# Another offset for the modulated input, merged small operations in the second attention, and a new schedule for the conditioning loads

## The chip, the cores and the metric

The kernel runs on one core of one Trainium2 chip, as a single launch. The metric is the time of one execution on the device in microseconds (us). A time is a median over several executions; for the kernel before it is 2225.2 us, the median of 3 runs (2223.86, 2225.2 and 2228.75). A profile is one further execution, recorded by the hardware profiler, with a time and a span of its own. The engines are named as the profile names them: PE is TensorE's matmuls and PEld its weight loads, DVE is VectorE, ACT is ScalarE, POOL is GpSimd, SP is SyncE.

## The reference, cut to what matters

A trunk of two layers over 256 positions of 2048 channels, all in float32. Layer 0 mixes positions with a forgetting attention of 16 heads of 128, layer 1 with a sliding-window attention of 32 query heads of 64 in pairs on 4 key heads, with one sink logit a head; after each stands a gated feed-forward with a causal convolution of width 3 (5632 wide). Every sub-layer is modulated by vectors that come from the conditioning vector c: shift and scale ahead of it, a gate behind it.

```python
def swa_attention(h, pos, w_in, sinks, w_o):
    ...
    sink = jnp.broadcast_to(sinks.astype(jnp.float32).reshape(1, 1, Hk, G, 1, 1), s.shape[:-1] + (1,))
    p = jax.nn.softmax(jnp.concatenate([s, sink], axis=-1), axis=-1)[..., :-1].astype(v.dtype)
    o = jnp.einsum('bnhgqk,bnkhd->bnqhgd', p, vb).reshape(B, S, Hq * dh)
    return o @ w_o
...
    c_act = jax.nn.silu(c)
    for i in range(DEPTH):
        mod = c_act @ ada_w[i] + ada_b[i]
        sh1, sc1, g1, sh2, sc2, g2 = jnp.split(mod[:, None, :], 6, axis=-1)
        h = x * (1.0 + sc1) + sh1
        ...
        x = layer_norm(DEEPNORM_ALPHA * x + (1.0 + g1) * y, ln_mix_g[i], ln_mix_b[i])
        h = x * (1.0 + sc2) + sh2
        y = conv_ffn(h, ffn_w_up[i], ffn_conv_w[i], ffn_conv_b[i], ffn_w_down[i])
        x = layer_norm(DEEPNORM_ALPHA * x + (1.0 + g2) * y, ln_ffn_g[i], ln_ffn_b[i])
    return x
```

## The kernel before, in words

**Matmuls.** Every float32 operand of a large matmul is split into a high part (rounded to the matmul's own format) and the remainder. The product of two operands is then three matmuls: high by high, high by low, low by high. mm() (line 75) issues each of them, so nearly all of TensorE's rows in the profile have line 75 and are told apart by tile names: wh and wl are the two parts of a weight tile, hH and hL those of the modulated input h, gT those of the feed-forward's hidden values, oT those of the attention's output; ws and xs are the results.

**Weights.** stream() (from line 256) brings the weights in tiles of 512 KB, two blocks of 128 rows by 512 columns: a DMA on SP's queue (line 261), ScalarE's rounding copy to wh (264), VectorE's subtraction to wl (275). It queues a "go" for each tile, which runs two tiles later and issues that tile's matmuls: 24 of 128x256 where the weights are the stationary operand (w_stationary, tile ws, with hH and hL moving: the up-projections and the first attention's queries and keys), or 12 of 128x512 where the activations are (x_stationary, tile xs: the other projections, with hH as a stationary operand in the second attention's input projection). then() puts other work into the same queue in its order, such as a change of a rate or the step between two sub-layers. Each go first runs one step of every deferred evacuation (run_post), and ends with tick(): the conditioning planner, and one step of the background work (later(), step(), drain()).

**hH and hL** share one buffer, hpad (line 483). hH begins 40 floats (160 bytes) into it and hL follows; hpad itself begins at a multiple of 256 bytes in its partition. Weight tiles, gT, oT and the like lie 224 bytes behind such a multiple.

**turn()** (326 to 329) issues four transposes of the identity into a bank that nobody reads. w_stationary calls it once, ahead of the third weight tile, in the first column block of each sub-block of a feed-forward: for the first sub-block it's in the second of the block's two projections, for the second sub-block in the first.

**The conditioning planner** works through the vectors in the order of ada_list (374); (l, v) is layer l and v of 0 to 5, where 2 and 5 are gates (used as rows) and the others columns. Its rate is a number of calls per weight tile; ada_tick() adds it to a debt and calls ada_step() for each whole one. ada_vector() (from 380) needs 32 calls that each issue a load of 512 KB (398) on SP's queue and one step on VectorE over 128x1024 (402 or 404). A gate then needs 5 calls more (with 2 ahead, one with its bias load on POOL), in which TensorE sums over the partitions and ScalarE copies (412 to 416). A column vector needs 4 calls that each transpose four pieces (442) and let ScalarE sum along them (446), and 2 that finish it (HELD, with another way, is empty). ada_need() calls ada_step() as often as it takes until a vector is there.

**Rates.** First feed-forward: 0.64 in the up-projections, 0.78 in the down-projections, second feed-forward 0.4 in both. Second attention: 0.3 for its keys and values (set behind between()), then 0.9 to the end of its output projection. The first attention's output projection: 1.3.

**between()** (from 1132) stands ahead of each sub-layer but the first: ada_need for shift and scale, spin() (some matmuls that nobody reads, to bridge a gap), then modulate(): normalise() (652, 654), transposes, and mod_pair() (503 to 508), which writes hH and hL. In residual() (626 to 643) the two blocks of 128 rows are added to x, with bn_stats and, on GpSimd, the power of -1/2.

**The second attention.** swa() (from 974) projects keys and values, then four groups of queries; evac_q() (1004 to 1023) rotates and transposes a group and hands its four pairs of heads to the background work; there are 16 pairs in all. A pair() (from 1025) computes the scores of both heads, calls probs() for each, turned() (three transposes and a copy to pT, 727 to 733) for each, and multiplies by the values; its result goes to an o_tile (the last four are hH's and hL's own blocks 12 to 15). probs() (692 to 713) takes the maximum (VectorE), two exponentials with sums (ScalarE), with a sink the exponential es of the sink (ScalarE) and its addition to ss (VectorE), the reciprocal (VectorE), and two scalings of pr by it (ScalarE, line 713: one 128 wide, one 256 wide). The first attention calls probs() too, without a sink. Its yields mark the steps that the background work is spread over. out_proj() (from 744) follows, with a wait in stat() that runs background steps until the o_tile that it needs is there.

**conv_ffn()** (from 1065) handles its 11 column blocks in two sub-blocks of 6 and 5: up-projection with convolution (1072 to 1075), silu and product, then the down-projection of the sub-block. Ahead of the first down-projection the background work is drained; ahead of each, ada_need asks for the gate.

Of the kernel before, what the change touches and what calls it, by code (L numbers as in the profile page):

```python
# [10 lines left out]
F32 = mybir.dt.float32  # L11
# [30 lines left out]
def hybrid_trunk(ctx: ExitStack, tc: tile.TileContext, a: dict, out: bass.AP):  # L42
# [283 lines left out]
    def turn():  # L326
        o = bank("turn")
        for j in range(4):
            pin(nc.tensor.transpose(o[:, j * P:(j + 1) * P], ident, ident))

    def w_stationary(wsrc, col, turn_at=-1):

        ps = w_banks()

        def use(kc, h, l):
            if kc == turn_at:
                turn()
            w_mm(ps, kc, h, l)

        stream(wsrc, 0, col, list(range(KC)), use)  # L340
        return ps
# [142 lines left out]
    hH, hL = (hpad[:, 40 + a * KC * S:40 + (a + 1) * KC * S].rearrange("p (k s) -> p k s", s=S) for a in range(2))  # L484
# [207 lines left out]
    def probs(S_ps, skc=None, nskc=None):  # L692

        regs = ((0, P), (P, 3 * P))
        nm = sp.tile([P, 2], F32, tag="nm", name="nm")
        pr = f32(gtile("pr")).rearrange("p a b -> p (a b)")[:, :3 * P]
        ss = sp.tile([P, 2], F32, tag="ss", name="ss")
        for r, (b, e) in enumerate(regs):

            mk = mask[:, 2:3, :] if r == 0 else (mask[:, 0::2, :] if skc is None else mask[:, 1:3, :])  # L700
            nc.vector.tensor_tensor_reduce(pr[:, b:e].rearrange("p (a k) -> p a k", k=P),
                                           S_ps[:, b:e].rearrange("p (a k) -> p a k", k=P), mk, -1.0,
                                           -NEG if skc is None else nskc, ALU.add, ALU.min, nm[:, r:r + 1])
        for r, (b, e) in enumerate(regs):
            nc.scalar.activation(pr[:, b:e], pr[:, b:e], AF.Exp, bias=nm[:, r:r + 1], scale=-1.0,
                                 accum_out=ss[:, r:r + 1])
        if skc is not None:
            es = sp.tile([P, 2], F32, tag="es", name="es")
            nc.scalar.activation(es, nm, AF.Exp, bias=skc)
            nc.vector.tensor_tensor(ss, ss, es, op=ALU.add)  # L710
        nc.vector.reciprocal(ss, ss)
        for r, (b, e) in enumerate(regs):
# [3 lines left out]
    def attend(scores, outputs, sinks=()):  # L716
# [4 lines left out]
        pr = probs(sps, *sinks)  # L721
# [22 lines left out]
    def out_proj(oT, full, w_o, l):  # L744
# [11 lines left out]
        for i, ks in enumerate((range(0, 8), range(8, 12))):  # L756
            then(lambda i=i: ada.update(rate=((1.3, 1.3, 1.3, 1.3), (0.9,) * 4)[l][i]))
            for d in range(2):
                part(d, list(ks))
        then(lambda: ada_need(l, 2))  # L760
        for d in range(D // WB):
            if d < 2:
                part(d, list(range(12, KC)))
            else:
                then(lambda d=d: ada.update(rate=((1.3, 1.3, 1.3, 1.3), (0.9,) * 4)[l][d]))
# [208 lines left out]
    def swa(l, j):  # L974
# [50 lines left out]
        def pair(g, n, q):  # L1025
# [11 lines left out]
            yield  # L1037
            prs, pTs = [], []
# [148 lines left out]
```

## Time and profile before

| | |
|---|---|
| median of 3 runs | 2225.2 us (2223.86 to 2228.75) |
| profiled execution | 2228.91 us |
| its span | 2227.1 us |
| mean granted TensorE clock | 0.992 |
| TensorE matmul busy | 2174.6 us, 98% |
| TensorE weight load busy | 1981.6 us, 89% |
| VectorE busy | 1778.1 us, 80% |
| ScalarE busy | 1167.2 us, 52% |
| GpSimd busy | 19.0 us, 1% |
| read from HBM | 598.37 MB, 270 GB/s |

The span is the time from the first to the last recorded instruction; the execution's own time is 1.8 us longer. Busy times are sums over the span, of one profiled execution. Matmuls run in a pipeline, so a matmul's recorded duration is longer than the time from one to the next; the rate is read from their number in a stretch. The stages on the span's clock: opening to 188 us, first attention's projections to 378, its output projection to 478, modulation to 500, first feed-forward: up to 747, down to 880, up to 1103, down to 1208; second attention: input projections from 1215 to 1364, output projection to 1481, modulation to 1518; second feed-forward: up to 1755, down to 1886, up to 2104, down to 2214; the rest is the last normalising and the output.

### The profile page before, as it was taken

How to read it: one execution, taken by the hardware profiler on the slowest of the kernel's cores; microseconds unless marked ns; L12 is line 12 of the kernel's file. 1: busy time of each engine (PE TensorE's matmuls, PEld its weight loads, DVE VectorE, ACT ScalarE, POOL GpSimd, SP SyncE). 2: the span in 40 equal slices, each digit the busy share in tenths (PEclk: the TensorE clock that was granted, in tenths of full speed). 3: DMA queues.
4: the chain of work that ended last, by engine and by line, in shares of the span. 5: the costliest groups of instructions: out<-in, count | busy, mean ns of one | idle time of the engine just before them, and what ended most of it. 6: DMA issues, size and time to landing. Idle time of an engine off the chain costs nothing. (4 is left out here: it accounts for less than half of the span.)

```text
span 2227.1 us, 38402 instructions
## 1 busy us (share of the span) xinstructions
PE 2174.6 (98%) x14931; PEld 1981.6 (89%) x14931; DVE 1778.1 (80%) x2426; ACT 1167.2 (52%) x1873; POOL 19.0 (1%) x48
## 2 busy tenths in 40 slices
PE   6999999999999999999999999999999999999997
PEld 5999888889999988999987777789999888999986
DVE  6978999979979968789888988769888555666756
ACT  3435655555555543555634578745555533555532
POOL 0000000000000000000000000000000000000000
PEclk9999999999999999999999999999999999999999
DMA  9999999969979989889887877658888566666663
GB/s 334 377 349 356 349 349 329 328 225 327 347 249 315 317 287 341 272 289 327 276 305 288 281 237 235 217 170 297 270 273 266 183 195 191 194 193 196 193 192 110
DMA packets 274248, 603.00 MB, mean 271 GB/s; under 512 B 21063, under 2 KB 29961, under 8 KB 273553
## 3 DMA queue, kind: packets, MB, share of 16 engines
q1 hardware_dynamic: 273008, 595.85, 78.8%
q0 software_dynamic: 1056, 4.69, 0.6%
q8 instruction: 117, 1.92, 0.3%
q14 instruction: 67, 0.54, 0.1%
HBM read 598.37 MB, written 2.10 MB: 270 GB/s over the span
## 5 line engine op out<-in xcount | busy, mean ns | idle before, releaser
L264 ACT CAST wh<-w 128x1024 fp32r<-128x1024 f32 x728 | 766.4, 1054 | 789.3 <-PE ws L75 279.7
L275 DVE TENSOR_TENSOR wl<-w,wh 128x1024 fp32r<-128x1024 f32 x728 | 888.6, 1223 | 353.4 <-ACT wh L264 342.8
L75 PE MATMUL ws<-hH,wh 128*128 128x256 f32 x6656 | 1157.6, 279 | 4.6 <-ACT hH L84 2.1
L75 PEld LDWEIGHTS ws<-hH,wh 128*128 128x128 f32 x6656 | 1012.7, 189 | 11.9 <-issue 3.6
L75 PE MATMUL ws<-hH,wl 128*128 128x256 f32 x3328 | 922.1, 278 | 3.1 <-DVE wl L275 3.0
L75 PEld LDWEIGHTS ws<-hH,wl 128*128 128x128 f32 x3328 | 628.9, 189 | 4.2 <-DVE wl L275 4.1
L75 PE MATMUL xs<-wh,gT 128*128 128x512 f32 x1408 | 435.7, 390 | 0.0
L75 PEld LDWEIGHTS xs<-wh,gT 128*128 128x128 f32 x1408 | 264.3, 188 | 54.8
L75 PE MATMUL xs<-wl,gT 128*128 128x512 f32 x704 | 273.9, 389 | 0.0
L75 PE MATMUL xs<-wh,hH 128*128 128x512 f32 x704 | 237.0, 402 | 0.1
L404 DVE SCALAR_TENSOR_TENSOR acc<-wa,cact,acc 128x1024 f32<-128x1024 f32 x180 | 228.7, 1279 | 0.0
L404 DVE SCALAR_TENSOR_TENSOR acc<-wa,cactp,acc 128x1024 f32<-128x1024 f32 x128 | 162.8, 1281 | 0.0
L75 PEld LDWEIGHTS xs<-wh,hH 128*128 128x128 f32 x704 | 131.3, 189 | 29.4 <-issue 1.5
L75 PEld LDWEIGHTS xs<-wl,gT 128*128 128x128 f32 x704 | 132.2, 188 | 27.2
L75 PE MATMUL xs<-wl,hH 128*128 128x512 f32 x352 | 139.6, 397 | 2.1 <-DVE wl L275 2.0
L1072 ACT ACTIVATE u<-ws,ccol 128x256 f32<-128x256 f32 x176 | 97.3, 564 | 58.1 <-PE ws L75 44.9
L75 PE MATMUL xs<-wh,oT 128*128 128x512 f32 x384 | 126.2, 399 | 0.0
L1073 DVE SCALAR_TENSOR_TENSOR u<-ws,ccol,u 128x255 f32<-128x255 f32 x176 | 82.9, 479 | 16.0 <-ACT u L1072 15.7
L75 PEld LDWEIGHTS xs<-wh,oT 128*128 128x128 f32 x384 | 72.9, 190 | 15.7 <-DVE oT L85 0.4
L1075 DVE SCALAR_TENSOR_TENSOR u<-ws,ccol,u 128x254 f32<-128x254 f32 x176 | 83.5, 479 | 2.1
L75 PEld LDWEIGHTS xs<-wl,hH 128*128 128x128 f32 x352 | 66.5, 189 | 16.7 <-DVE wl L275 3.6
L573 DVE SCALAR_TENSOR_TENSOR oacc<-wo,cact,oacc 128x1024 f32<-128x1024 f32 (+1 forms) x68 | 73.4, 1079 | 8.2 <-DMA wo<-in_ada_w_dram 7.0
(213 smaller groups left out, 1290.0 us busy)
## 6 DMA issues: line engine op xcount, KB each, us to landing
w<-in_ffn_w_up_dram SPq DMA_DIRECT2D x352, 512.0 KB, 4.8
wa<-in_ada_w_dram SPq DMA_DIRECT2D x320, 512.0 KB, 5.5
w<-in_ffn_w_down_dram SPq DMA_DIRECT2D x176, 512.0 KB, 4.3
w<-in_fox_w_in_dram SPq DMA_DIRECT2D x96, 512.0 KB, 7.0
wo<-in_ada_w_dram SPq DMA_DIRECT2D x48, 512.0 KB, 8.9
w<-in_swa_w_in_dram SPq DMA_DIRECT2D x40, 512.0 KB, 5.2
w<-in_fox_w_o_dram SPq DMA_DIRECT2D x32, 512.0 KB, 6.4
w<-in_swa_w_o_dram SPq DMA_DIRECT2D x32, 512.0 KB, 4.9
```

The lines of the kernel that those rows point to most:

```text
L75: return nc.tensor.matmul(o, lhsT, rhs, start=start, stop=stop, **kw)
L264: pin(nc.scalar.copy(h, w), False)
L275: pin(nc.vector.tensor_tensor(l, w, f32(h), op=ALU.subtract), behind[0] > 0)
L404: pin(nc.vector.scalar_tensor_tensor(ac, wo, (cactp if row else cact)[:, k:k + 1], ac, op0=ALU.mult, op1=ALU.add), True)
L573: nc.vector.scalar_tensor_tensor(acc, w[:, k], cact[:, kc:kc + 1], acc, op0=ALU.mult, op1=ALU.add)
L1072: nc.scalar.activation(u, pf, AF.Identity, bias=cw(CW, f), scale=cw(2, f))
L1073: nc.vector.scalar_tensor_tensor(u[:, 1:], pf[:, :S - 1], cw(1, f), u[:, 1:], op0=ALU.mult, op1=ALU.add)
L1075: nc.vector.scalar_tensor_tensor(u[:, 2:], pf[:, :S - 2], cw(0, f), u[:, 2:], op0=ALU.mult, op1=ALU.add)
```

## The change

It has three parts.

1. hH's offset in hpad is now set by place(): 20 floats (80 bytes) for the first attention and both feed-forwards, 56 floats (224 bytes) for the second attention, called in between() behind the two ada_need. Against the 224 bytes at which weight tiles lie, 80 bytes are 144 less, and 224 are the same place. turn() and its calls are removed.
2. In the second attention, es, its addition to ss and the reciprocal are done once for both heads of a pair, on tiles of 128x4, where they were done once a head on 128x2. The addition of the sink's logit, so far the bias of es's exponential, becomes a VectorE operation of its own. Of the two scalings of a head the 128-wide one goes to VectorE (tensor_scalar_mul); the 256-wide one stays on ScalarE. A pair has two yields more.
3. The rates: 0.85 for 0.78 in the first feed-forward's down-projections; in the second attention 0.8 for 0.9 behind the keys and values, 0.3 from the second group of queries on and in the output projection until gate (1, 2) is there, 0.6 after it. The first attention's stay at 1.3.

```diff
--- before.py
+++ after.py
@@ -323,21 +323,10 @@
         stream(wsrc, k0, col, list(range(nk)), use)
         return ps
 
-    def turn():
-        o = bank("turn")
-        for j in range(4):
-            pin(nc.tensor.transpose(o[:, j * P:(j + 1) * P], ident, ident))
-
-    def w_stationary(wsrc, col, turn_at=-1):
+    def w_stationary(wsrc, col):
 
         ps = w_banks()
-
-        def use(kc, h, l):
-            if kc == turn_at:
-                turn()
-            w_mm(ps, kc, h, l)
-
-        stream(wsrc, 0, col, list(range(KC)), use)
+        stream(wsrc, 0, col, list(range(KC)), lambda kc, h, l: w_mm(ps, kc, h, l))
         return ps
 
 
@@ -481,7 +470,13 @@
 
 
     hpad = cst.tile([P, 2 * KC * S + 64], F32R, name="hH")
-    hH, hL = (hpad[:, 40 + a * KC * S:40 + (a + 1) * KC * S].rearrange("p (k s) -> p k s", s=S) for a in range(2))
+    hH = hL = None
+
+    def place(o):
+        nonlocal hH, hL
+        hH, hL = (hpad[:, o + a * KC * S:o + (a + 1) * KC * S].rearrange("p (k s) -> p k s", s=S) for a in range(2))
+
+    place(20)
 
     def mod_turn(k, n=1):
 
@@ -689,36 +684,37 @@
         return G, B
 
 
-    def probs(S_ps, skc=None, nskc=None):
-
-        regs = ((0, P), (P, 3 * P))
-        nm = sp.tile([P, 2], F32, tag="nm", name="nm")
+    REGS = ((0, P), (P, 3 * P))
+
+    def exps(S_ps, nm, ss, nskc=None):
+
         pr = f32(gtile("pr")).rearrange("p a b -> p (a b)")[:, :3 * P]
-        ss = sp.tile([P, 2], F32, tag="ss", name="ss")
-        for r, (b, e) in enumerate(regs):
-
-            mk = mask[:, 2:3, :] if r == 0 else (mask[:, 0::2, :] if skc is None else mask[:, 1:3, :])
+        for r, (b, e) in enumerate(REGS):
+
+            mk = mask[:, 2:3, :] if r == 0 else (mask[:, 0::2, :] if nskc is None else mask[:, 1:3, :])
             nc.vector.tensor_tensor_reduce(pr[:, b:e].rearrange("p (a k) -> p a k", k=P),
                                            S_ps[:, b:e].rearrange("p (a k) -> p a k", k=P), mk, -1.0,
-                                           -NEG if skc is None else nskc, ALU.add, ALU.min, nm[:, r:r + 1])
-        for r, (b, e) in enumerate(regs):
+                                           -NEG if nskc is None else nskc, ALU.add, ALU.min, nm[:, r:r + 1])
+        for r, (b, e) in enumerate(REGS):
             nc.scalar.activation(pr[:, b:e], pr[:, b:e], AF.Exp, bias=nm[:, r:r + 1], scale=-1.0,
                                  accum_out=ss[:, r:r + 1])
-        if skc is not None:
-            es = sp.tile([P, 2], F32, tag="es", name="es")
-            nc.scalar.activation(es, nm, AF.Exp, bias=skc)
-            nc.vector.tensor_tensor(ss, ss, es, op=ALU.add)
+        return pr
+
+    def probs(S_ps):
+
+        nm, ss = (sp.tile([P, 2, 2], F32, tag=n, name=n)[:, 0, :] for n in ("nm", "ss"))
+        pr = exps(S_ps, nm, ss)
         nc.vector.reciprocal(ss, ss)
-        for r, (b, e) in enumerate(regs):
+        for r, (b, e) in enumerate(REGS):
             nc.scalar.mul(pr[:, b:e], pr[:, b:e], ss[:, r:r + 1])
         return pr
 
-    def attend(scores, outputs, sinks=()):
+    def attend(scores, outputs):
 
         sps = bank("S")
         scores(sps)
         yield
-        pr = probs(sps, *sinks)
+        pr = probs(sps)
         yield
         pT = turned(pr)
         yield
@@ -754,15 +750,14 @@
             stream(w_o, 0, d * WB, ks, use)
 
         for i, ks in enumerate((range(0, 8), range(8, 12))):
-            then(lambda i=i: ada.update(rate=((1.3, 1.3, 1.3, 1.3), (0.9,) * 4)[l][i]))
+            then(lambda i=i: ada.update(rate=(1.3, 0.3)[l]))
             for d in range(2):
                 part(d, list(ks))
-        then(lambda: ada_need(l, 2))
+        then(lambda: (ada_need(l, 2), ada.update(rate=(1.3, 0.6)[l])))
         for d in range(D // WB):
             if d < 2:
                 part(d, list(range(12, KC)))
             else:
-                then(lambda d=d: ada.update(rate=((1.3, 1.3, 1.3, 1.3), (0.9,) * 4)[l][d]))
                 ps[d] = x_banks()
                 part(d, list(range(KC)))
             then(lambda d=d: defer(residual(ps[d], d, gates[l, 2], True)), d == D // WB - 1)
@@ -1035,9 +1030,23 @@
                         mm(o[:, r * P:(r + 1) * P + r * P], qx[rr, qs], kx[rr, ks], start=m == 0, stop=m == 2,
                            skip_group_check=True)
             yield
+            nm, ss, es = (sp.tile([P, 2, 2], F32, tag=n_, name=n_) for n_ in ("nm", "ss", "es"))
             prs, pTs = [], []
             for i in range(2):
-                prs.append(probs(sps[i], sink[:, h + i:h + i + 1], nsink[:, h + i:h + i + 1]))
+                prs.append(exps(sps[i], nm[:, i, :], ss[:, i, :], nsink[:, h + i:h + i + 1]))
+                yield
+            nc.vector.tensor_tensor(es, nm, sink[:, h:h + 2].rearrange("p (i o) -> p i o", o=1).broadcast_to([P, 2, 2]),
+                                    op=ALU.add)
+            nc.scalar.activation(es, es, AF.Exp)
+            nc.vector.tensor_tensor(ss, ss, es, op=ALU.add)
+            nc.vector.reciprocal(ss, ss)
+            for i in range(2):
+                for r, (b, e) in enumerate(REGS):
+                    o = prs[i][:, b:e]
+                    if r == 0:
+                        nc.vector.tensor_scalar_mul(o, o, ss[:, i, r:r + 1])
+                    else:
+                        nc.scalar.mul(o, o, ss[:, i, r:r + 1])
                 yield
             for i in range(2):
                 pTs.append(turned(prs[i]))
@@ -1055,8 +1064,10 @@
         ps = x_stationary(w_in, KOFF, 0, KC, hstat)
         for t in range(NT):
             then(lambda t=t, ps=ps: defer(evac_kv(t, ps[t])))
-        then(lambda: (ada.update(rate=0.9), bg.update(gap=2)))
+        then(lambda: (ada.update(rate=0.8), bg.update(gap=2)))
         for g in range(SKV):
+            if g == 1:
+                then(lambda: ada.update(rate=0.3))
             ps = x_stationary(w_in, g * WB, 0, KC, hstat)
             then(lambda g=g, ps=ps: defer(evac_q(g, ps)))
         out_proj(oT, full, w_o, l)
@@ -1104,10 +1115,10 @@
             gT = []
             then(lambda: ada.update(rate=(0.64, 0.4)[l]))
             for b in range(b0, b1):
-                ps = w_stationary(w_up, b * WB, 4 if b == b0 > 0 else -1)
+                ps = w_stationary(w_up, b * WB)
                 sil = [ttile("sil") for _ in range(2)]
                 then(lambda ps=ps, b=b, sil=sil: defer(evac(ps, b * 4, silu(sil))))
-                ps = w_stationary(w_up, DFF + b * WB, 4 if b == 0 else -1)
+                ps = w_stationary(w_up, DFF + b * WB)
                 then(lambda ps=ps, b=b, sil=sil, gT=gT: defer(evac(ps, DFF // P + b * 4, gated(sil, gT))))
 
             def stat(kc, t, gT=gT):
@@ -1119,7 +1130,7 @@
                 if si == 0:
                     drain()
                 ada_need(l, 5)
-                ada["rate"] = (0.78, 0.4)[l]
+                ada["rate"] = (0.85, 0.4)[l]
 
             then(ready)
             for d in range(D // WB):
@@ -1133,6 +1144,7 @@
 
         ada_need(l, v)
         ada_need(l, v + 1)
+        place(20 if v else 56)
         o = bank("spin")
         release()
         spin(o, 3)
```

## The prediction

> **What bounds the kernel now.** I read the page's head first, then its groups, then the busy time by stage. Columns of the last: stretch, its length, busy time (instructions) by engine, granted TensorE clock, DMA share, GB/s.
>
> ```profile
> span 2227.1 us, 38402 instructions
> PE 2174.6 (98%) x14931; PEld 1981.6 (89%) x14931; DVE 1778.1 (80%) x2426; ACT 1167.2 (52%) x1873; POOL 19.0 (1%) x48
> ```
> ```profile
> 747.00:880.00 133.00, 133.00 (x599) 110.14 (x598) 108.17 (x111) 59.67 (x88) 0.00 (x0) 1.00 0.90 315
> 1240.00:1364.00 124.00, 122.67 (x669) 94.56 (x667) 103.64 (x244) 87.47 (x210) 0.00 (x0) 1.00 0.79 255
> 1364.00:1450.00 86.00, 82.98 (x452) 63.08 (x451) 66.18 (x157) 63.13 (x181) 0.58 (x1) 0.98 0.68 222
> 1481.00:1518.00 37.00, 35.59 (x288) 33.65 (x286) 34.81 (x54) 25.25 (x36) 1.11 (x2) 1.00 0.52 168
> 1886.00:2104.00 218.00, 218.00 (x1923) 217.96 (x1923) 140.11 (x188) 115.03 (x153) 0.00 (x0) 1.00 0.62 193
> ```
> TensorE sets the end in every stage that the change touches. In the last up-projection (1886 to 2104) matmuls and weight loads both fill the whole stretch. The second attention (1240 to 1450) is TensorE too, with small holes, and VectorE 84% busy beside it.
>
> **The rate of one matmul.** Next I asked for the up-projection's tile alone, and for its groups in two of these stretches.
>
> ```profile
> 267.00:281.00 14.00, 14.00 (x120) 13.95 (x119) 0.00 (x0) 0.00 (x0) 1.00 1.01 380
> 880.00:886.00 6.00, 5.81 (x48) 5.63 (x48) 0.00 (x0) 0.00 (x0) 1.00 0.93 326
> 1509.00:1516.00 7.00, 7.00 (x61) 6.97 (x60) 0.96 (x2) 1.14 (x2) 1.00 0.74 224
> 1520.00:1720.00 200.00, 200.00 (x1768) 200.00 (x1767) 35.76 (x76) 20.49 (x37) 1.00 0.84 283
> 1890.00:2100.00 210.00, 209.81 (x1850) 209.63 (x1850) 32.81 (x72) 19.86 (x36) 1.00 0.62 194
> ```
> ```profile
> L75 PE MATMUL ws<-hH,wh 128*128 128x256 f32 x80 | 14.2, 281 | 0.0
> ```
> ```profile
> L75 PE MATMUL ws<-hH,wh 128*128 128x256 f32 x1233 | 209.9, 276 | 0.0
> ```
> The same instruction has two speeds: 210/1850 = 113.4 ns apart when one lasts 276 ns, and 14/120 = 117 to 118 when it lasts 281. Operands, shapes and clock are the same; only what ran just before differs. I call them fast and slow. Slow costs 4.4 ns a matmul. turn() is what flips it:
>
> ```profile
> 885.53 0.28 PE L75 MATMUL ws<-hH,wl 128*128 128x256 f32 x1
> 885.65 0.60 PE L329 MATMUL turn<-ident 128*128 128x128 f32 x4
> 886.00 0.48 PE L75 MATMUL ws<-hH,wh 128*128 128x256 f32 x2
> ```
> Slow before it (880 to 886), fast after.
>
> **Part 1, the offset and turn().** Without turn() the gap 885.53 to 886.00 (0.47, less one step of 0.11) and a slower first step go: 0.45 us, four times, **-1.8 us**. The offset's own effect is in no row: hH stands 160 bytes past a multiple of 256 now, 80 afterwards (224 in the second attention). Bounds: weight loads fill 217.96 of 218.00 us, and their operands stay where they are, so fast cannot become faster; at best all is fast. Where fast isn't steady already,
>
> ```profile
> 188.00:378.00 190.00, 100.76 (x812) 96.86 (x812) 8.84 (x13) 0.00 (x0) 1.00 0.97 341
> ```
> there are these 812 in the first attention, and a block of 192 after each of the two barriers into an up-projection: 1196 times 4.4 is 5.3 us if all are slow now. At worst the slow speed holds everywhere: 8448 up-projection matmuls times 4.4 = +37. In the second attention hH is the stationary operand:
>
> ```profile
> L75 PE MATMUL xs<-wl,hH 128*128 128x512 f32 x8 | 3.2, 394 | 0.0
> ```
> ```profile
> L75 PE MATMUL xs<-wl,oT 128*128 128x512 f32 x24 | 9.3, 389 | 0.0
> ```
> There the new offset is the one at which oT lies, and oT's matmul is 5 ns shorter on one form in three: 480 x 5/3 = 0.8 us. I take 3.2 + 0.8 = **-4 us**: nearer the good end, because the fast speed holds in the longest stretches.
>
> A rule of the Trainium skill speaks against this term: "SBUF — State Buffer", section "Who interferes with whom", gives TensorE two independent read ports and says that PE and ACT never wait on anyone. By it an address would be no lever, this term 0 and the sum below +5.7. The two speeds of one instruction above are not what it leads one to expect, but they don't show that the address is the cause; so it is rival 2.
>
> **Part 2, the second attention.** Per pair of heads ScalarE loses one es and two 128-wide scalings; VectorE loses one sum and one reciprocal and gains one small sum and two 128-wide scalings.
>
> ```profile
> L713 ACT ACTIVATE pr<-pr,ss 128x128 f32<-128x128 f32 x48 | 19.3, 402 | 16.0 <-DVE ss L711 15.9
> L709 ACT ACTIVATE es<-nm,sink 128x2 f32<-128x2 f32 x32 | 9.1, 284 | 0.0
> L711 DVE RECIPROCAL ss<-ss 128x2 f32<-128x2 f32 x48 | 7.8, 162 | 1.8 <-ACT pr L705 1.2
> L654 DVE TENSOR_SCALAR x<-x,mv,rs 128x512 f32<-128x512 f32 x12 | 5.7, 542 | 2.1 <-POOL rs L642 2.1
> ```
> ScalarE: 284 + 2 x 402 = 1.09 us less, 16 pairs: 17 us. VectorE's 128-wide scaling is in no row; it lies between 162 (2 wide) and 542 (512 wide), and I take 0.30, nearer the small one: 2 x 0.30 - 0.16 = 0.44 us more a pair, 7 us in all. None of this is TensorE time; it counts through TensorE's holes alone:
>
> ```profile
> 1390.59 0.39 PE L75 MATMUL xs<-wh,oT 128*128 128x512 f32 x1
> 1391.94 0.55 PE L730 MATMUL T<-ident,pr 128*128 128x128 f32 x3 [0.96 <-ACT pT L732]
> ```
> ```profile
> 1394.50:1397.80 3.30, 3.30 (x9) 2.62 (x9) 3.13 (x9) 2.92 (x9) 0.00 (x0) 0.50 0.82 266
> ```
> This is the worst: 1.1 us of hole, two of 0.6 behind it, then half the clock for 3.4 us. By the busy times, holes are 1.3 us (1240 to 1364) and 3.0 (1364 to 1450), and the half clock costs 1.7: 6.0. A matmul's mark of 0.39 over a step of 0.22 (133.0/599) hides 0.17 of each hole; with some twenty holes the bounds are 0 and -9. I take **-5 us**, a little over half, as conditioning leaves VectorE too. A pair now takes 8 background steps where it took 6, so the last two pairs need four forced steps at the end of the queue where two were forced: +1 inside the -5. The new sum waits for ScalarE's es; behind it on VectorE stand the wl subtractions that TensorE reads two tiles later. That wait exists now, 32 times; it becomes 16. The first attention's instructions stay as they are, and place() issues none.
>
> **Part 3, the conditioning.** Each call of the planner adds one 512 KB load on SP's queue and one 1.28 us VectorE step, until 32 are done; a column vector then needs 4 transposing calls and 2 to end (38), a gate 39. Counting calls by the rates gives 181 in the first feed-forward now (96 x 0.64 + 48 x 0.78 + 80 x 0.64 + 40 x 0.78), 153 for the four vectors ahead of gate (1,2), so 26 of its 32 steps by 1215. The rows by stage confirm it (columns: VectorE, this line alone; a column's first two steps are another line):
>
> ```profile
> 1103.00:1215.00 112.00, 33.12 (x26) 1.00 0.89 312
> 1215.00:1242.00 27.00, 3.83 (x3) 1.00 0.64 194
> 1242.00:1364.00 122.00, 26.85 (x21) 1.00 0.79 255
> 1364.00:1418.00 54.00, 14.06 (x11) 0.97 0.70 221
> 1418.00:1481.00 63.00, 1.28 (x1) 1.00 0.61 203
> ```
> 3 + 3 + 26 finish the gate; 2 + 18 + 11 + 1 finish vector (1,4) with its last step some 60 us ahead of the barrier. With the new rates: 187 calls in the feed-forward finish the gate's 32 steps (cost 0: VectorE is 108 of 133 us busy beside a full TensorE in 747 to 880; without that cover 6 x 1.28 = 7.7). The gate's 5 last calls and 38 for (1,4) are 43 calls for the second attention, which brings 8 x 0.3 + 8 x 0.8 + 36 x 0.3 + 20 x 0.6 = 31.6. So **about 12 calls are left** when between() asks for (1,4): 6 steps, 4 transposing calls, the end, all at once, with nothing for TensorE beside them. They are pinned on VectorE behind the last residual:
>
> ```profile
> 1483.63 0.16 DVE L641 TENSOR_SCALAR mv<-mv 128x1 f32<-128x1 f32 x1
> ```
> ```profile
> 1480.96 2.10 PE L75 MATMUL spin<-mask,ident 128*128 128x384 f32 x6
> 1485.61 1.46 PE L75 MATMUL spin<-mask,ident 128*128 128x384 f32 x4
> 1486.61 0.70 PE L75 MATMUL ws<-hH,wh 128*128 128x256 f32 x2
> ```
> ```profile
> L404 DVE SCALAR_TENSOR_TENSOR acc<-wa,cact,acc 128x1024 f32<-128x1024 f32 x180 | 228.7, 1279 | 0.0
> L446 ACT ACTIVATE sm<-sm 128x128 f32<-128x128 f32 x96 | 25.3, 264 | 5.7 <-PE sm L442 4.1
> L446 ACT ACTIVATION_READ_ACCUMULATOR sm<-sm 128x1 f32 x96 | 18.5, 193 | 0.0
> ```
> From 1483.8: five steps of 1.28 until the first half of acc is whole (1490.2; the sixth runs beside what follows), transposes 0.5, sixteen ScalarE sums of 264 + 193 less their 0.04 overlap, 6.6, then four small VectorE operations of 0.16 and their hand-overs, 0.8: 1498.1. Now the modulation starts 1.1 ahead of the first ws, at 1485.5. The shift is **+12.6 us**; then one stretch at half clock as after 1394.5, **+1.7**. The transposes and sums that leave the second attention save TensorE 4 x 0.45: **-1.8**. The gate's bias load on POOL comes earlier and nothing waits for it. Six loads stand on SP's queue ahead of up-projection weights; the DMA engines are at 0.52 there and have time.
>
> **Sum**: -1.8 - 4 - 5 + 12.6 + 1.7 - 1.8 = +1.7. The profiled execution took 2228.9 (span 2227.1, 1.8 around it) and becomes 2230.6; it lies 3.7 over the median of the runs, 2225.2, which becomes **2226.9**.
>
> **The rivals.** 1 (forecast): all parts as worked out; by the bounds of parts 1 and 2, 2220 to 2232. Chance 0.42.
>
> 2, slower: **the offset doesn't hold the fast speed**, and nothing flips it any more. For: it was slow in three of the four sub-blocks when turn() came (880 and 1509 above, and the row below), and undisturbed it stays.
>
> ```profile
> 1886.00:1891.50 5.50, 5.45 (x47) 5.46 (x48) 0.00 (x0) 0.00 (x0) 1.00 0.61 187
> ```
> It decides if slow outlives the first column block. Price at 4.4 ns: the 1768 and 1850 matmuls of the rows from 1520 and 1890, 7.8 and 8.1 us, and half of the 1920 in the first layer's second sub-block, 4.2; the 4 us of part 1 are not won: 2226.9 + 24 = 2251. Chance 0.17.
>
> 3, slower by a little: **the holes of the second attention stay** (they end on the wh casts and pT copies, not on what was removed): +5, 2232. Against it: ScalarE's own waits for ss (15.9 us above). Chance 0.17.
>
> 4, faster: **the barrier doesn't get the 12 calls**, because the planner is further than my count or the steps run under the residual: without 12.6 and 1.7, 2212.6. Against: the count fits five rows. Chance 0.24.
>
> **How the numbers follow.** About 0.2% (4.5 us) can be told from no change. Faster: rival 4 and a tenth of case 1, 0.28. Same: most of case 1 and a little of rival 3, 0.35. Slower: rival 2, most of 3, the upper tail of 1, 0.37. The range goes from inside rival 4 to short of rival 2's time, 2211 to 2246; case 1 alone is 2220 to 2232.
>
> **What would show it.** Part 1: every 1920-matmul stretch at 113.4 and 276 ns, also right after an interruption. Part 2: no half clock near 1394; fewer waits of pr for ss. Part 3: six L404-type steps in one row with no matmul between, and ws starting some 17 us after the last xs instead of 5.7. I am wrong if that gap stays below 8 us, or if ws shows 281 ns in a long stretch.

## The result, and the profile after

The changed kernel takes **2225.89 us**, the median of 20 runs (2223.03 to 2229.99), against 2228.19 for the kernel before, median of 20 runs taken beside them. The ratio is 0.9988, with a 95% interval of 0.9979 to 0.9997. That is 0.1% faster: inside the 0.2% that I called no change and inside my range, but below one by its whole interval, where I had forecast 1.7 us more. The sign was wrong.

The head of the page of the changed kernel:

```profile
span 2224.4 us, 38328 instructions
PE 2168.7 (97%) x14915; PEld 1973.9 (89%) x14915; DVE 1785.4 (80%) x2442; ACT 1152.5 (52%) x1825; POOL 19.9 (1%) x48
```

TensorE is still the bound. The two spans are 2.8 us apart, and behind that stand terms of 10 us of both signs. I took the start of the first matmul of each stage from the traces; the differences are the stages' durations (us, one profiled execution each; the first attention ends with its last xs, "down, second half" and "second attention" go from their first to the end of their last xs, "gap" from there to the first ws):

| stage | before | after | e1 | e2 | e3 | e4 | e6 | e13 |
|---|---|---|---|---|---|---|---|---|
| opening | 186.96 | 185.16 | 182.56 | 185.23 | 184.98 | 183.12 | 187.05 | 184.70 |
| first attention | 285.06 | 285.68 | 287.12 | 286.04 | 284.43 | 284.80 | 285.28 | 286.09 |
| up, first half (layer 0) | 270.02 | 269.73 | 269.66 | 269.83 | 269.83 | 269.67 | 269.65 | 269.68 |
| up, second half | 221.38 | 221.53 | 220.92 | 221.38 | 221.94 | 220.92 | 221.53 | 221.53 |
| down, second half | 109.59 | 109.00 | 109.57 | 109.59 | 108.99 | 109.58 | 109.00 | 109.00 |
| second attention | 264.72 | 254.42 | 263.93 | 260.98 | 260.26 | 260.84 | 255.25 | 255.81 |
| gap behind it | 5.49 | 16.05 | 5.48 | 5.49 | 15.15 | 5.49 | 5.49 | 5.49 |
| up, first half (layer 1) | 268.86 | 268.31 | 268.13 | 268.59 | 269.63 | 268.08 | 268.13 | 268.16 |
| up, second half | 218.26 | 217.64 | 217.64 | 218.27 | 218.26 | 217.64 | 217.64 | 217.64 |

The stages left out agree within 0.05 us. The second attention gains 10.3 us and the gap behind it takes 10.6 back. (Five later profiles of the kernel before, e11, e12 and e14 to e16 below, have 264.03 to 264.08 us in the second attention; against these the gain is 9.6.) First the gain: the whole second attention, before and then after, by the windows view (columns as in the prediction: stretch, its length, busy time and instructions of PE, PEld, DVE, ACT and POOL, granted clock, DMA share, GB/s).

```profile
1216.40:1481.10 264.70, 260.35 (x1371) 202.62 (x1370) 210.86 (x453) 177.59 (x423) 0.58 (x1) 0.99 0.72 231
```
```profile
1214.50:1468.90 254.40, 254.22 (x1354) 198.21 (x1352) 204.94 (x454) 159.09 (x343) 0.00 (x0) 1.00 0.66 213
```

TensorE was idle for 4.35 of 264.7 us before and for 0.18 of 254.4 after; the clock was granted in full. ScalarE has 18.5 us less to do: 13 of them left with the pair's new form (e2), 6 with the sums that now run behind the attention (e3).

Then the gap, by the timeline of the changed kernel:

```profile
1468.54 0.39 PE L75 MATMUL xs<-wh,hH 128*128 128x512 f32 x1
...
1471.52 6.06 DVE L393 SCALAR_TENSOR_TENSOR acc<-wa,cact,acc 128x1024 f32<-128x1024 f32 x5
...
1476.44 3.67 PE L431 MATMUL sm<-ident,acc 128*128 128x128 f32 x16 [7.51 <-DVE acc L393]
...
1477.59 0.26 ACT L435 ACTIVATE sm<-sm 128x128 f32<-128x128 f32 x1 [4.16 <-PE sm L431]
...
1482.69 0.18 DVE L417 SCALAR_TENSOR_TENSOR cv<-tot,acol 128x16 f32<-128x16 f32 x1 [3.28 <-ACT sm L435]
...
1484.98 0.69 PE L75 MATMUL ws<-hH,wh 128*128 128x256 f32 x2
```

This is the forced finish of vector (1, 4): five conditioning steps on VectorE right behind the residual, the sixteen transposes, sixteen sums on ScalarE from 1477.59 to 1482.6, and only then cv and the modulation. The last row of xs starts at 1468.54, the first ws at 1484.98.

### The profile page after: what moved, and what is told of

Same layout as the page of the kernel before. It is cut to its first block, busy times and chain, and to the rows that moved or that the text cites. A ratio compares the mean times of both kernels' runs of the same rounds, so it can differ in the third digit from the quotient of the medians.

```text
span 2224.4 us, 38328 instructions
## 1 busy us (share of the span) xinstructions
PE 2168.7 (97%) x14915; PEld 1973.9 (89%) x14915; DVE 1785.4 (80%) x2442; ACT 1152.5 (52%) x1825; POOL 19.9 (1%) x48
## 5 line engine op out<-in xcount | busy, mean ns | idle before, releaser
L75 PEld LDWEIGHTS xs<-wl,hH 128*128 128x128 f32 x352 | 66.5, 189 | 18.1 <-DVE wl L275 4.5
```

Of the source, the lines that this page charges most:

```text
L75: return nc.tensor.matmul(o, lhsT, rhs, start=start, stop=stop, **kw)
```

## The experiments

Ratios are against the kernel before on the same chip, with 95% intervals.

### e1: part 1 alone

```diff
-    hH, hL = (hpad[:, 40 + a * KC * S:...
+    place(20)            # between(): place(20 if v else 56)
-    turn() and its two calls
```

> Part 1 alone on the kernel before (new offsets, turn() removed). Theory A, the offset makes the fast speed come back by itself within some ten matmuls after each interruption: the four up-projection stretches last 269.7, 221.5, 268.3 and 217.6 us as in the changed kernel, the second attention gains under 1 us, total -1 to -3 us against the kernel before. Theory B, the offset does nothing and only luck kept the changed kernel fast: one or more of the stretches from 880, 1520 and 1890 is slow to its end at 117.8 ns a matmul, 8 us each, total +5 to +24 us.

Measured: 2224.75 us, ratio 0.9972 (0.9953 to 0.9992). The four stretches last 269.66, 220.92, 268.13 and 217.64 us, the second attention 263.93: 0.8 less than in the first profile of the kernel before, but only 0.1 less than in the five later ones (264.03 to 264.08), so no gain is shown there. Theory A holds in the stages; the median fell further, by 5.9 us, than the profile's stages say (2.2 in the up-projections). e14 to e16 show a likely reason.

### e2: part 2 alone

```diff
-                prs.append(probs(sps[i], sink..., nsink...))
+                prs.append(exps(sps[i], nm[:, i, :], ss[:, i, :], nsink[...]))
+            (es, ss and the reciprocal once for both heads; r == 0 scaled on VectorE)
```

> Part 2 alone on the kernel before (small operations once per pair, 128-wide scaling on VectorE, eight steps a pair). Theory A, these operations made TensorE's holes: the second attention (first to last xs) goes from 264.7 to about 258 us, total -5 to -7. Theory C, the holes came from the conditioning's VectorE steps and end with the rates: 264.7 becomes 263 or more, total 0 to -2.

Measured: 2226.54 us, ratio 0.999 (0.997 to 1.0009). The second attention takes 260.98, 3.7 less: between the theories. Its row, for the same stretch as above:

```profile
1214.60:1475.50 260.90, 257.25 (x1370) 200.52 (x1369) 216.74 (x469) 164.86 (x377) 0.58 (x1) 1.00 0.73 234
```

ScalarE lost 13 us of work, VectorE gained 6, and TensorE still has 3.65 us of holes of the 4.35. The stretch at half clock is gone too (mean clock 0.99 before, 1.00 here), but that isn't this part's doing: five of the six profiles of the kernel before and e1 have none in this stage either. These five take 264.06 us with 4.9 us of holes. Against them e2 gains 3.1 us, of which 1.3 is hole; the remaining 1.8 I can't assign.

### e3: part 3 alone

```diff
-        rate=0.9 from the keys and values to the end of out_proj; 0.78 in the first down-projections
+        rate=0.8, then 0.3 from group 1, 0.3 and 0.6 in out_proj; 0.85
```

> Part 3 alone on the kernel before (rates). Both theories: the last xs to the first ws behind the second attention goes from 5.5 to about 16 us, with five conditioning steps in a row on VectorE. Theory A: the second attention loses the transposes and sums (1.8 us) and little else, 264.7 to 262, total about +8. Theory C: it goes to 257, total about +3.

Measured: 2233.16 us; ratio 1.0001 (0.9977 to 1.0025), no difference shown by it. The second attention takes 260.26, 4.5 less and between the theories; the gap 15.15 instead of 5.49. Of the 4.5, 1.4 are the sixteen transposes that moved behind the attention (four of them in a row put 584 ns, instead of 230, between the starts of two xs matmuls). Again most holes stay:

```profile
1214.00:1474.00 260.00, 256.01 (x1353) 198.71 (x1351) 199.19 (x438) 171.22 (x391) 0.13 (x1) 1.00 0.64 209
```

### e4: parts 1 and 2, old rates

> The changed kernel with the old rates (parts 1 and 2 without 3). Both theories: the gap behind the second attention is 5 to 6 us again, 10.5 less than in the changed kernel. Theory A: the second attention lasts about 257 us where the changed kernel has 254.4, total -8 to -9 us against the kernel before, 0.996 of it, faster than the changed kernel. Theory C: it goes back to 263, total -2 to -3.

Measured: 2221.86 us, ratio 0.996 (0.9942 to 0.9977); gap 5.49, second attention 260.84. The total is as theory A has it, by luck: the 5.9 us of e1 weren't in it. The stage isn't: at the old rates the pair's new form is worth 3.1 us (e1 to e4), at the new ones 5 to 6 (e3 to the changed kernel, 5.8, of which part 1 has at most 0.8). So neither A nor C alone: each part by itself leaves about 4 us of holes, both together leave none. Both take work out of the stage in which TensorE waited; that it is the same waits which both shorten wasn't followed.

### e5: the old offset without turn()

> The kernel before without turn(), offset 40 as it was. Theory A (the offset is what keeps the changed kernel fast, and turn() did it before): each up-projection stretch that starts slow stays slow to its end: 880 to 1101 goes from 221.4 to about 229, 1486 to 1755 from 268.9 to about 276, 1886 to 2104 from 218.3 to about 226; the profiled execution is 16 to 25 us longer, and the times lie 10 to 25 us over the kernel before. Theory B (neither offset nor turn() decides; the speed is drawn by chance): about as many slow stretches as before, total -2 to +8 us.

Measured: 2244.81 us, ratio 1.0061 (1.0036 to 1.0085). The profiled execution's span is 2251.4: the four stretches last 278.20, 222.51, 277.45 and 226.13 us, 25.8 more than before. The last of them, the up-projection's tile alone (stretch, length, PE, PEld, DVE, ACT, clock, DMA, GB/s):

```profile
1910.00:2120.00 210.00, 210.00 (x1786) 210.00 (x1785) 32.76 (x72) 19.75 (x36) 1.00 0.65 187
```

And the changed kernel in the same stage:

```profile
1890.00:2098.00 208.00, 208.00 (x1837) 208.00 (x1837) 32.77 (x72) 19.77 (x36) 1.00 0.62 194
```

117.6 ns a matmul against 113.2, both with a full TensorE at full clock. e5 and e1 differ in the offset alone; their four stretches differ by 27.9 us together, their spans by 29.5. Theory B falls. Theory A holds in size, less in place: of the three stretches that it named, the last two stayed slow, and so did the first half of layer 0, which it hadn't named. The second stretch came back to the fast speed behind an interruption, four transposes of the conditioning at 935.0: at the old offset an interruption can change the speed, and it then stays until another one does.

### e6: parts 1 and 2 with rates that finish the conditioning

```diff
-        rate 0.8; 0.3 from group 1; out_proj 0.3, then 0.6
+        rate 0.8; 0.5 from group 1; out_proj 0.5, then 0.9
```

> The changed kernel with rates that bring 45 calls into the second attention instead of 32: 0.8 in the first group, 0.5 from the second on, 0.9 behind the gate. By my count of calls the vector (1, 4) is complete before the modulation: the gap behind the second attention is 5.5 us instead of 16.05. If the holes are a matter of how much VectorE work lies in the attention (theory C), the second attention gives back 4 to 6 of its 254.4 us, total -6 us against the changed kernel; if the pair's operations count (theory A), 1 to 3, total -8 to -9.

Measured: 2217.6 us, ratio 0.9942 (0.9919 to 0.9965). The second attention takes 255.25 us (0.8 more than in the changed kernel, less than either theory has), the gap 5.49. The conditioning's VectorE steps, first in the changed kernel and then in e6, same four stretches (stretch, length, busy time of this line, clock, DMA, GB/s):

```profile
1215.00:1242.00 27.00, 0.00 (x0) 1.00 0.51 156
1242.00:1364.00 122.00, 12.79 (x10) 1.00 0.67 213
1364.00:1418.00 54.00, 5.12 (x4) 1.00 0.52 163
1418.00:1481.00 63.00, 20.09 (x16) 0.93 0.80 275
```
```profile
1215.00:1242.00 27.00, 0.00 (x0) 1.00 0.50 149
1242.00:1364.00 122.00, 19.16 (x15) 1.00 0.73 233
1364.00:1418.00 54.00, 7.67 (x6) 1.00 0.60 190
1418.00:1481.00 63.00, 11.43 (x9) 1.00 0.72 242
```

The same 30 steps; e6 has seven of them earlier, and none behind the last xs. In the whole stage TensorE has no hole, although VectorE has 6 us more than in the changed kernel:

```profile
1215.50:1471.00 255.50, 255.50 (x1372) 199.98 (x1371) 210.87 (x464) 165.91 (x376) 0.58 (x1) 1.00 0.70 227
```

The clock's share of 0.93 in the changed kernel's last stretch falls into the wait for the conditioning. This run shows that the forced finish was what cancelled the gain.

### e7: other offsets

```diff
-    place(20); between(): place(20 if v else 56)
+    place(56); between(): place({(0, 3): 56, (1, 0): 20, (1, 3): 0}[l, v])
```

> The changed kernel with other offsets: 56 floats (224 bytes, the weights' own place) in the first attention and the first feed-forward, 20 (80 bytes) in the second attention, 0 in the second feed-forward. If the step of a stationary hH follows its place, the second attention's xs steps on hH go from 229.2 to 233 ns and the first attention's from 233.3 to 229, -2 us and +2 us. For a moving hH I expect at 224 the two speeds of before, without turn() slow to the end of a stretch (first feed-forward +8 in each half); at 0, unknown: 113.4 ns with or without a transient. If the place is no lever, all stretches stay within 0.5 us of the changed kernel's.

Measured, in one execution: span 2268.0 us, 43.6 more than the changed kernel. Up-projections: 282.87 and 233.86 us at 224 bytes, 278.24 and 224.00 at 0; second attention 256.77 at 80 (2.4 more). One form's durations (minimum, median, maximum), first at 224 bytes, then at 0 in the second half; behind them the same in the changed kernel, at 80:

```profile
L75 PE MATMUL ws<-hH,wl x616: 282/283/288, 894.9 to 1119.8; 128*128 128x256 f32 x154
```
```profile
L75 PE MATMUL ws<-hH,wl x601: 277/279/281, 1929.8 to 2139.8; 128*128 128x256 f32 x151
```
```profile
L75 PE MATMUL ws<-hH,wl x612: 275/275/275, 1889.9 to 2097.7; 128*128 128x256 f32 x153
```

By the distance of consecutive starts (those under 130 ns) the steps are 120.0, 116.7 and 113.35 ns. At 0 there is a second step. The first half of layer 1 lies there too, and from 1536 to 1762 it runs at another one (the tile's row, columns as in e5):

```profile
1540.00:1760.00 220.00, 220.00 (x1871) 220.00 (x1870) 36.34 (x78) 21.31 (x39) 1.00 0.83 270
```

220/1871 is 117.6 ns, by the starts 117.8; behind the next interruption, at 1762, it is 116.7. The place is a lever, of 6%. My expectation for 224 was wrong: not two speeds but one, slower than both. A stationary hH goes the other way: its xs steps (means of the distances under 245 ns) were 233.3 in the opening and the first attention at 80 and 229.0 at 224, in the second attention 229.2 at 224 and 233.2 at 80, as expected. In the first attention's rows, changed kernel and then e7, minimum and median are higher at 80:

```profile
L75 PE MATMUL xs<-wl,hH x22: 391/394/503, 245.4 to 263.9; 128*128 128x512 f32 x22
```
```profile
L75 PE MATMUL xs<-wl,hH x22: 387/390/500, 245.5 to 263.7; 128*128 128x512 f32 x22
```

The first attention as a whole gained nothing from 224 (285.78 against 285.68), because its ws steps went to 119.8 there.

### e8, e9: two details of the pair

```diff
e8:                 nc.scalar.mul(o, o, ss[:, i, r:r + 1])   # for both r
e9: -                yield      # behind each head's exps()
```

> The changed kernel with both scalings of a head on ScalarE again; the merged small operations and the added steps stay. If the 128-wide scaling's move to VectorE is what closed holes, the second attention goes from 254.4 to 256.5 or more; if the merged sums and reciprocals did, it stays within 1 us of 254.4.

> The changed kernel without the two added yields of a pair (both heads' exponentials in one background step, six steps a pair as before). If spreading the work over more steps closed holes, the second attention goes from 254.4 to 256 us or more; if only the number of operations counts, it stays within 0.7 us of 254.4.

Measured, in one execution each: the second attention takes 256.15 us in e8, 1.7 more than in the changed kernel, so the move of the scaling has part of the gain, under the 2.1 that I had set as its mark. In e9 it takes 252.66, 1.8 *less*: neither expectation.

### e10: e6's rates without part 2

> The rates of e6 (0.8, 0.5, 0.5, 0.9) and part 1, with the pair as it was before (part 2 undone). e6 has 255.25 us in the second attention and a gap of 5.49. If the pair's operations are worth what they were worth alone in e2 (3.7 us), it takes 259 us; if the slower conditioning leaves room enough for them, under 257.

Measured, in one execution: the second attention takes 261.34 us, more than both expectations. With the pair's new form (e6) it's 255.25, so this form is worth 6.1 us at these rates, more than the 3.7 alone. Without it the holes are back (257.93 of 261.5 us busy), at fewer VectorE microseconds than in e6:

```profile
1213.00:1474.50 261.50, 257.93 (x1371) 200.81 (x1371) 206.25 (x447) 177.89 (x424) 0.58 (x1) 1.00 0.68 222
```

So the sum of VectorE's work isn't what makes a hole (206.25 us with holes, 210.87 without). The form of the pair is: the hand-overs between the two engines, or ScalarE's 12 us more (177.89 against 165.91). Two other runs speak for the hand-overs: e8 and e3 have the same rates and ScalarE 167.8 and 171.5 us busy in the stage, but 0.8 and 3.8 us of holes. They differ in more than the hand-overs, so this isn't settled.

### e11, e12, e14, e15, e16: the kernel before again

> The kernel before once more, for its spread: some of its executions take 10 us more than most. If these are executions in which an up-projection stays slow behind turn(), a profile of one has one of the four stretches 7 to 9 us longer at 117.8 ns a matmul; an execution near 2226 has all four within 0.7 us of the first profile's (270.0, 221.4, 268.9, 218.3).

> As e11: the kernel before once more. A long execution has one of the four up-projection stretches 7 to 9 us longer, or, if the spread comes from elsewhere (the opening, the transfers), another stage of it is longer.

> The kernel before a fourth time, to catch one of its long executions (2234 to 2248): if such a one is an up-projection that stays slow behind turn(), one of the four stretches is 7 to 9 us longer at 117.8 ns a matmul; if another stage is longer, this theory falls. An execution near 2226 tells nothing.

> As e14: one of the four up-projection stretches 7 to 9 us longer in a long execution, or another stage, and then this theory falls. An execution near 2226 tells nothing.

> As e14: one of the four up-projection stretches 7 to 9 us longer in a long execution, or another stage, and then this theory falls. An execution near 2226 tells nothing.

These five took 2226.83, 2223.54, 2231.21, 2226.31 and 2234.17 us. Three have all four up-projections as in the first profile. The two longest have one long one each: 278.26 instead of 270.02 us (e14, first half of layer 0), 278.08 instead of 268.86 (e16, first half of layer 1). In e14 it starts at a wait for a weight tile, long behind turn() (503.2):

```profile
519.96 0.39 PE L75 MATMUL ws<-hH,wh 128*128 128x256 f32 x2
521.13 0.38 PE L75 MATMUL ws<-hH,wl 128*128 128x256 f32 x1 [0.78 <-DVE wl L275]
```

From there to the end of the stretch the step is the slow one. In the same execution the next stretch is fast (windows on the up-projection's tile):

```profile
530.00:745.00 215.00, 213.82 (x1798) 212.14 (x1798) 36.76 (x78) 20.40 (x37) 1.00 0.88 299
890.00:1100.00 210.00, 208.84 (x1831) 207.80 (x1830) 33.67 (x72) 19.85 (x36) 1.00 0.88 297
```

213.82/1798 is 118.9 ns against 114.1 (both with their few interruptions). In e16 the stretch is slow from 1505.5 on, and turn() at 1513.7 doesn't change it:

```profile
1520.00:1755.00 235.00, 233.82 (x1969) 232.15 (x1967) 39.23 (x84) 22.58 (x41) 1.00 0.80 260
```

Of 89 timed executions of the kernel before, 35 lie over 2232 us, up to 2247.7. Of the 61 of the five kernels with parts 1 and 2 or part 1 alone (changed kernel, e1, e4, e6, e13), none does; the widest of them spreads over 8.0 us. That a slow stretch lies behind each long execution isn't shown: two were profiled, and none over 2234.17. At the new offset the profiles show no slow stretch: after most interruptions six to fourteen steps of 114 to 121 ns, then 113.

What an interruption does at the old offset depends on its kind. This is counted in the nine profiles at that offset (the six of the kernel before, e2, e3, e5), wherever at least ten steps stand on each side of the interruption. TensorE's sums for a gate never changed the speed, 72 of 72. Behind turn() it was fast 31 times of 32, behind the conditioning's transposes 56 of 56; behind the modulation's transposes it was slow 25 times of 90, behind a wait 7 of 29. So turn() did its work, but a wait behind it could undo it.

### e13: e6 with six steps a pair

> e6 without the two added yields of a pair: parts 1 and 2 with six steps a pair, rates 0.8, 0.5, 0.5 and 0.9. If the added steps cost in themselves what e9 showed (1.8 us in the second attention), it takes 253.5 us instead of e6's 255.25 with the gap still 5.5: total about 2 us below e6. If e9's gain came from something that only the starved rates allow, it stays within 0.7 us of e6.

Measured: 2216.27 us, ratio 0.9939 (0.9919 to 0.9959), the lowest median of all, but not distinguishable from e6. The second attention takes 255.81, within 0.7 of e6: e9's 1.8 us, seen in one execution where the conditioning is starved, don't show here, and the added steps cost nothing.

## Why the prediction was wrong

**Each part went in the direction forecast; the sizes of parts 2 and 3 were wrong, and part 1 got its size for another reason.** "-1.8 - 4 - 5 + 12.6 + 1.7 - 1.8 = +1.7". The step that failed is what parts 2 and 3 do together. The sum gave them -5 - 1.8 + 12.6 + 1.7 = +7.5 us. From e1, which has part 1 alone, to the changed kernel they are +1.1 in the profiles (-9.5 in the second attention, +10.6 in the gap). In the medians it is 1.1 too (2224.75 and 2225.89, not measured side by side). The base moved as well: the kernel before, 2225.2 us in its three runs, took 2228.19 in twenty, with some long executions among them (below). Against the 2225.2 the changed kernel's 2225.89 would be 0.7 slower. So it is these two together, the sizes and a base of three runs, that turned the sign. That the changed kernel came within 1.0 us of the 2226.9 forecast for it is luck: the errors of the terms cancelled.

In the two profiles: up-projections -1.3, second attention -10.3, gap +10.6, first attention +0.6, second half of the first down-projection -0.6 (a term that I didn't have; e3 shows it with the rates alone), opening -1.8. The opening spreads from 182.6 to 187.0 us over profiles of the same kernel before, so its -1.8 shows nothing of the change.

**Part 3: +12.6 + 1.7 measured +10.6.** The count of calls held: vector (1, 4) was short, its rest ran as one block behind the residual, and the gap was 16.05 us where I had said some 17 (the sum's own 12.6 on top of 5.5 makes 18.1). Five forced steps instead of six. The sixteen sums took 5.1 us, not 6.6: ScalarE starts one every 0.28 us (0.4 four times), where I had added the durations of both halves less 0.04. And the half clock cost nothing: it fell on the wait itself.

```profile
1469.00:1480.00 11.00, 3.56 (x17) 3.57 (x18) 10.30 (x15) 6.26 (x20) 2.00 (x2) 0.65 0.49 152
1480.00:1483.50 3.50, 3.50 (x11) 1.98 (x11) 0.61 (x4) 2.62 (x18) 0.58 (x1) 0.65 1.05 423
1483.50:1487.00 3.50, 3.50 (x25) 2.97 (x24) 2.87 (x8) 2.50 (x5) 0.00 (x0) 1.00 0.40 162
```

0.65 while TensorE had only transposes and the spin matmuls, 1.00 again ahead of the first ws.

**Part 2: -5, with -1.8 and -0.8 for the same stage, measured -10.3 in sum, -9.5 from e1.** The term that failed is "I take -5, a little over half". The holes closed altogether: the 9.5 less the 1.4 of the transposes are 8.1 of the 9 us that I had as the far bound. That bound held 1.7 us for the half clock behind 1394.5, which is no rule: five of the six profiles of the kernel before don't have it, and are only 0.7 us shorter in this stage. The working had part 2 and the conditioning's leaving as one term with a discount; e2, e3 and e10 show that they enhance each other. The durations were near: the 128-wide scaling on VectorE took 283 ns where I took 300; es once a pair is 202 ns, and ScalarE still waits for ss, now on the wider scaling (13.5 us):

```profile
L1049 ACT ACTIVATE pr<-pr,ss 128x256 f32<-128x256 f32 x32 | 14.7, 502 | 13.5 <-DVE ss L1042 13.5
L1047 DVE TENSOR_SCALAR pr<-pr,ss 128x128 f32<-128x128 f32 x32 | 7.8, 283 | 0.5
L1040 ACT ACTIVATE es<-es 128x4 f32<-128x4 f32 x16 | 3.2, 202 | 0.8 <-DVE es L1038 0.6
```

I had named ScalarE's waits for ss, 15.9 us, as the evidence against rival 3. They are of both attentions; the second alone, from 1210 to 1482 in the kernel before, has 12.0, in 12 waits:

```profile
L713 ACT ACTIVATE pr<-pr,ss 128x128 f32<-128x128 f32 x32 | 12.8, 400 | 12.0 <-DVE ss L711 12.0
```

The changed kernel waits there oftener and longer, 15 times and 13.5 us against 12 times and 12.0, where I had named fewer waits as a sign of part 2. What closed was TensorE's waiting.

**Part 1: -5.8 measured -1.3 to -2.2 in the up-projections of one profile, -0.1 to -0.8 in the second attention, about 0 in the first.** The 0.8 that I had for the second attention isn't shown: at 224 bytes its xs steps on hH are 229.2 ns in the changed kernel, but 230.0 in e1 and 229.6 in e4, and they were 229.6 at 160. The 5.3 us bound counted the first attention's matmuls, and left out that hH is a stationary operand there too: its 300 xs steps went from 229.5 to 233.1 ns, 1.1 us, which is what its ws steps gave back (from 115.7, 116.5 and 114.8 ns in its three blocks to 114.4, 114.2 and 115.0). But my sum was made on one execution of the kernel before in which turn() had done its work. I took its rows for the rule; e14 and e16 show executions in which the fast speed is lost behind turn() or doesn't come back with it, each 8 to 9 us longer. Over many runs part 1 is worth -5.9 us (e1; by the ratio's interval -1.8 to -10.5). That this is the size which I gave it is luck, since I gave it for another reason.

**Rival 2** had the wrong condition, and its price was right by luck: without turn() and at the old offset the span grew by 24.2 us (e5), and I had worked out 24. Its terms were others: 4.2 for the second half of layer 0 (measured 1.1), 4 for what part 1 doesn't win, and nothing for the first half of layer 0 (8.2). The medians are 16.3 apart. And the new offset holds the fast speed. The rule of the Trainium skill that I weighed beside it, in "SBUF — State Buffer", section "Who interferes with whom", gives TensorE's two reads independent ports; by it e1 and e5 would take the same time. They differ by 27.9 us in the four up-projections, so here the measurement decides against what I had drawn from it. **Rival 4** didn't come true in the changed kernel, since its barrier did get the calls; e6, which takes them away, is 2217.6, 10.9 under the median of the kernel before beside it (the rival: 12.6 under).

That the place of hH decides the step is shown (e1, e5, e7). Why it does is not: no run tells whether the distance to the weights' place counts or the place itself, since the weights lay at 224 in all of them. Why the old form of the pair makes holes at less VectorE work (e10) was read from busy times only, not followed wait by wait, and stays open, as does why fewer steps help in e9 and not in e13.

## What to carry to other kernels

When a schedule is moved out of a busy stage, count to the barrier that needs its end: here some eleven calls too few (five steps, four that transpose, two that end it) took back 10.6 us, all of the second attention's 10.3, and rates that finish in time (0.8, 0.5, 0.5, 0.9) kept 9.5 of them. Take several profiles before you call a row the rule, above all when the times of one kernel fall into groups: the group that you didn't profile may hold the gain. And where one matmul form shows two durations at full clock, try its moving operand at another place in its partition.

## What the runs showed of the hardware

With the weights 224 bytes behind a multiple of 256, the time from one float32 matmul of 128x256 to the next depended on where its moving operand began (bytes behind a multiple of 256, full clock in all):

| moving operand at | step | seen in |
|---|---|---|
| 80 | 113.3 ns, after six to fourteen slower ones behind most interruptions | changed kernel, e1, e4, e6, e8 to e10, e13 |
| 160 | 113.3 or 117.8 ns, lastingly, until an interruption changes it | kernel before (six profiles), e2, e3, e5 |
| 0 | 116.7 or 117.8 ns | e7, one execution |
| 224 | 120.0 ns | e7, one execution |

As the stationary operand of a 128x512 matmul the same buffer is worst of the three places tried at 80 (233.2 to 233.3 ns). At 224 it took 229.0 to 230.0 and at 160 229.6 to 229.7; these two aren't told apart. I hadn't expected that the place which is best for one role is the worst for the other.
